# First stage of a convolution and SwiGLU block: modulation vectors and token scaling moved from TensorE and VectorE to ScalarE, a new written order, and a bank of its own for the last half tile

## The chip, the cores and the metric

The kernel runs on one core of one Trainium2 chip. The core has five engines with instruction queues of their own: TensorE (PE, matrix products into PSUM banks), VectorE (DVE), ScalarE (ACT), GpSimd (POOL) and SyncE (SP, which here only issues transfers). Each queue is worked through in order; an instruction waits for semaphores that others raise. The metric is the device time of one execution in microseconds (us), as a median of runs.

## The reference

One layer (DEPTH is 1) over 1024 tokens of width 1024, in float32:

```python
sh1, sc1, g1, sh2, sc2, g2 = split(silu(c) @ ada_w + ada_b, 6)   # 1024 values each
h  = rmsnorm(x, norm1_g) * (1 + sc1) + sh1
gate_b, gate_c, hv = split(h @ conv_w_in, 3)                     # 1024 x 3072
y  = (gate_b * conv3_grid(gate_c * hv, conv_w)) @ conv_w_out
x  = x + g1 * y
h2 = rmsnorm(x, norm2_g) * (1 + sc2) + sh2
gate, up = split(h2 @ ffn_w_in, 2)                               # 1024 x 5632
x  = x + g2 * ((silu(gate) * up) @ ffn_w_out)
out = rmsnorm(x, final_g)
```

## The kernel before

Every large product is done on operands of the type that the profile calls fp32r, each split into a high part (a cast, on ACT) and a low part (the rest, a subtraction on DVE): three matmuls stand for one, high x high, low x high and high x low (TERMS). The large products also use a Strassen-like scheme with seven instead of eight block products, which is why tiles are called P1 to P7, S1 to S4, 11, 12, 21 and 22.

**The first stage** is what the change is about. It makes `sh1` and `sc1`, and with them the first products of `h @ conv_w_in`, for the first 512 tokens and for seven output blocks of 128 columns (the pairs in EARLY), each in a PSUM bank of its own (tile `x` in the profile). It goes through the width in eight steps, k = 0 to 7, of 128 rows of the product. Step k needs

- `ada[k]`: the 1024 rows of `ada_w` for 128 entries each of shift and scale, 1 MB, loaded on SP's queue in four transfers (`Ada.load`). Its sum over 8 blocks of rows, weighted with silu(c), is made in two accumulators: blocks 0 and 1 on ACT (`ada_acc`, L161), the others on DVE (L165), one addition of the two accumulators (L77), and the rest on PE: `total` sums over partitions by matmuls of one column (L179), of the merged accumulator (`ones`) and, from k = 1, of block 7 left out of the sums (`direct`; the factor is then a column of `cols`). Two entries, shift and scale, make 4 matmuls per step, and the profile shows each as two.
- `columns` (L184, L186, on DVE): scale1 and shift1, 128 values each, from the PSUM result.
- the token values of the step: xT is modulated with them, `A11h` or `A12h` (high, on ACT, L729), `xT` again in full precision (DVE, L314) and `A11l` or `A12l` (low, DVE, L74).
- the weights `w0r` (458 KB, SP's queue) and their parts `w0h` (ACT, L358) and `w0l` (DVE, L74).

The stage's order is written out by hand, for PE, ACT, DVE and SP: a loop over k, in which a list of (pair, terms) sets the order of the 21 matmuls. `by_term` does seven pairs' high x high, then seven low x high, then seven high x low; after the fourteenth (n == 14) the next step's `total` and `tokens` are written, so that they run while PE does the last seven. Steps 3 and 7 use `by_half`, with `total` earlier. After step 3 the seven banks hold P1, which ACT copies out (`save_p1`, L372) and POOL's queue stores to memory (`aside`, L373). Loads for step k+3 are issued at the start of step k; after the loads of the eight steps come the other 512 tokens (x) and the weights `wf` of five more blocks. PE then goes on without a break in those blocks (L410) and in the stage called Mixes (L460).

**The end.** The last product P4 is accumulated in four banks (`zs`). Three token tiles are finished first; the fourth, in `LastTile`, is done in two halves of 256 columns, both in the same bank, so that the first half's scaling runs beside the second half's matmuls. `rest` then takes the root of the sum of squares (`rsqrt`: ACT's root, and a Newton step on DVE), scales both halves of the row and writes them.

## Time and profile before

| | |
|---|---|
| median of 3 runs | 1000.98 us (1000.25 to 1001.6) |
| profiled execution | 1000.51 us, its span 998.7 us |
| PE busy | 983.7 us, 98% of the span, 4426 matmul records |
| DVE, ACT, POOL busy | 718.4, 482.3, 102.7 us |
| DMA, mean over the span | 181 GB/s |
| first stage (16.6 to 66.4 us): PE, DVE, ACT busy | 48.7, 41.0, 29.1 of 49.8 us |

The page counts an engine as busy while it computes; of a 998.7 us span PE is idle for 15.0 us. Rows of the timeline give start, length, engine, line, operation, tiles, and in brackets how long the engine stood idle before the instruction and what ended that.

### The profile page before, as it was taken

How to read it: one execution, taken by the hardware profiler on the slowest of the kernel's cores; microseconds unless marked ns; L12 is line 12 of the kernel's file. 1: busy time of each engine (PE TensorE's matmuls, PEld its weight loads, DVE VectorE, ACT ScalarE, POOL GpSimd, SP SyncE). 2: the span in 40 equal slices, each digit the busy share in tenths (PEclk: the TensorE clock that was granted, in tenths of full speed). 3: DMA queues.
4: the chain of work that ended last, by engine and by line, in shares of the span. 5: the costliest groups of instructions: out<-in, count | busy, mean ns of one | idle time of the engine just before them, and what ended most of it. 6: DMA issues, size and time to landing. Idle time of an engine off the chain costs nothing.

```text
span 998.7 us, 12313 instructions
## 1 busy us (share of the span) xinstructions
PE 983.7 (98%) x4426; PEld 809.2 (81%) x4426; DVE 718.4 (72%) x1038; ACT 482.3 (48%) x766; POOL 102.7 (10%) x183
## 2 busy tenths in 40 slices
PE   8999999999999999999999999999999999999996
PEld 6788888887788878888888888888888888888885
DVE  5877988888746799787665665665665755878885
ACT  6555876675435675243333333333334353535553
POOL 2131001110111210110110110110110110000000
PEclk9999999999999999999999999999999999999999
DMA  9997489996784232545431431431316954577533
GB/s 298 321 349 243 135 260 268 279 296 194 242 235 148 85 107 84 161 156 153 133 116 53 148 116 53 146 108 63 127 56 211 376 196 155 176 261 277 185 123 133
DMA packets 155325, 180.46 MB, mean 181 GB/s; under 512 B 8020, under 2 KB 112576, under 8 KB 155264
## 3 DMA queue, kind: packets, MB, share of 16 engines
q1 hardware_dynamic: 141584, 135.81, 43.5%
q0 software_dynamic: 12448, 40.69, 12.7%
q10 hardware_dynamic: 1232, 3.18, 0.8%
q8 instruction: 34, 0.56, 0.2%
q14 instruction: 27, 0.22, 0.1%
HBM read 135.33 MB, written 38.03 MB: 174 GB/s over the span
## 4 chain that ended last, share of the span: by engine, by line
PE 93%; DVE 2%; DMA 2%; ACT 1%; issue 1%; POOL 0%; ACTq 0%; DVEq 0%; POOLq 0%
PE X_f L570 23%; PE zP L1384 21%; PE m L460 16%; PE Z_f L570 12%; PE y L1014 7%; PE Y_f L570 6%; PE x L368 3%; PE x L410 3%; PE xT L295 1%; DMA vl_t<-vd 1%; PE ada_ps L179 1%; PE x1T L987 1%; DMA rows<-in_norm_g_dram 1%; DMA wr_f<-in_ffn_w_in_dram 1%; PE ada_ps L244 0%
## 5 line engine op out<-in xcount | busy, mean ns | idle before, releaser
L74 DVE TENSOR_TENSOR BP_f<-wr_f,BP_f 128x512 fp32r<-128x512 f32 x154 | 105.0, 687 | 60.7 <-ACT BP_f L83 58.8
L83 ACT CAST BP_f<-wr_f 128x512 fp32r<-128x512 f32 x154 | 94.2, 620 | 87.0 <-PE Z_f L570 55.9
L1384 PE MATMUL zP<-w3l_P,a3h_P 128*128 128x512 f32 (+1 forms) x319 | 121.8, 382 | 0.0
L1384 PE MATMUL zP<-w3h_P,a3l_P 128*128 128x512 f32 (+1 forms) x319 | 121.8, 382 | 0.0
L1384 PE MATMUL zP<-w3h_P,a3h_P 128*128 128x512 f32 (+1 forms) x319 | 120.4, 382 | 0.6 <-DVE bot L80 0.6
L1384 PEld LDWEIGHTS zP<-w3h_P,a3h_P 128*128 128x128 f32 x319 | 60.0, 188 | 12.5 <-DVE bot L80 0.8
L1384 PEld LDWEIGHTS zP<-w3h_P,a3l_P 128*128 128x128 f32 x319 | 60.0, 188 | 11.6
L1384 PEld LDWEIGHTS zP<-w3l_P,a3h_P 128*128 128x128 f32 x319 | 60.0, 188 | 11.5
L74 DVE TENSOR_TENSOR a3l_P<-a3l_P,a3h_P 128x1024 fp32r<-128x1024 f32 (+1 forms) x42 | 47.4, 1134 | 24.8 <-ACT a3h_P L1239 24.8
L570 PE MATMUL X_f<-A11h,BP_f 128*128 128x512 f32 x176 | 57.7, 390 | 0.0
L570 PE MATMUL X_f<-AS3h,BP_f 128*128 128x512 f32 x176 | 57.7, 389 | 0.0
L570 PE MATMUL Z_f<-AS4h,BP_f 128*128 128x512 f32 x176 | 57.6, 389 | 0.0
L570 PE MATMUL X_f<-AS2h,BP_f 128*128 128x512 f32 x176 | 57.6, 389 | 0.0
L570 PE MATMUL X_f<-A22h,BP_f 128*128 128x512 f32 x176 | 57.6, 389 | 0.0
L570 PE MATMUL Y_f<-A12h,BP_f 128*128 128x512 f32 x176 | 57.5, 389 | 0.0
L570 PE MATMUL Z_f<-AS1h,BP_f 128*128 128x512 f32 x176 | 57.4, 389 | 0.0
L1014 PE MATMUL y<-woh,vh_t 128*128 128x512 f32 x128 | 50.5, 394 | 0.0
L1014 PE MATMUL y<-woh,vl_t 128*128 128x512 f32 x128 | 49.9, 390 | 0.0
L1014 PE MATMUL y<-wol,vh_t 128*128 128x512 f32 x128 | 49.9, 390 | 0.0
L1239 ACT CAST a3h_P<-a3l_P 128x1024 fp32r<-128x1024 f32 (+1 forms) x42 | 40.7, 978 | 14.4 <-DMA a3l_P<-ad_S 7.9
L74 DVE TENSOR_TENSOR wr_f<-wr_f,wr_f 128x512 f32<-128x512 f32 x66 | 45.2, 688 | 1.5
L77 DVE TENSOR_TENSOR u_f<-Z_f,u_f 128x512 f32<-128x512 f32 x22 | 15.2, 690 | 37.5 <-ACT u_f L587 34.8
(310 smaller groups left out, 2331.9 us busy)
## 6 DMA issues: line engine op xcount, KB each, us to landing
wr_f<-in_ffn_w_in_dram SPq DMA_DIRECT2D x44, 512.0 KB, 4.4
ada_w<-in_ada_w_dram SPq DMA_DIRECT2D x64, 256.0 KB, 6.0
w_P<-in_ffn_w_out_dram SPq DMA_DIRECT2D x30, 512.0 KB, 5.9
a3l_P<-ad_S SPq DMA_DIRECT2D x20, 512.0 KB, 6.4
ad<-a POOLq DMA_DIRECT2D x33, 256.0 KB, 2.6
ada_w<-in_ada_w_dram SPq DMA_DIRECT2D x16, 512.0 KB, 4.8
a3l_P<-ad SPq DMA_DIRECT2D x15, 512.0 KB, 3.9
wr<-in_conv_w_in_dram SPq DMA_DIRECT2D x12, 512.0 KB, 6.2
```

The costliest lines, as they stand in the source:

```text
L74: return nc.vector.tensor_tensor(o, a, b, op=ALU.subtract)
L77: return nc.vector.tensor_tensor(o, a, b, op=ALU.add)
L83: nc.scalar.copy(hi, raw)
L179: nc.tensor.matmul(self.ps[j][:, j:j + 1], lhsT=part[:, j, :], rhs=by, start=i == 0, stop=i == n - 1)
L295: nc.tensor.transpose(self.ps[g][:, i * P:(i + 1) * P], self.x[:, k * P:(k + 1) * P], ident)
L368: nc.tensor.matmul(xbank[pair], lhsT=w0[k][wi][:, place[pair], :], rhs=h_of(k, 0)[hi], start=(k == 0 and i == 0), stop=(k == KD - 1 and i ...
L410: nc.tensor.matmul(xbank[self.pair], lhsT=self.w[wi][:, k, :], rhs=h_of(half * KH + k, 0)[hi], start=(half == 0 and k == 0 and i == 0), st ...
L460: nc.tensor.matmul(self.ps[a], lhsT=self.w[pname][wi][:, k, a * P:(a + 1) * P], rhs=A[aname, k // 2][hi][:, k % 2, :], start=(q == 0 and k ...
L570: mm = nc.tensor.matmul(ps, lhsT=w[:, wi, 2 * kp + kk, :], rhs=A[aname, kp][hi][:, kk, :], start=(first and kp == 0 and kk == 0 and i == 0 ...
L1014: mm = nc.tensor.matmul(ys[t][n], lhsT=vt[t][vi][:, k, :], rhs=wo[k][wi][:, n * H:(n + 1) * H], start=(k == 0 and i == 0), stop=(k == KD - ...
L1239: nc.scalar.copy(hi, f(lo))
L1384: mm = nc.tensor.matmul((zs[t] if to is None else to)[:, cols], lhsT=a[ai][:, k % 2, t * P:(t + 1) * P], rhs=w[wi][:, k % 2, cols], start= ...
```

## The change

In the first stage:

- `Ada` is made with `direct` 2 for k = 1 and 0 for the later steps (1 before): step 1 has 6 one-column matmuls instead of 4, steps 2 to 7 have 2 each. The block of rows that PE no longer sums is one more instruction on DVE (L165 before, L167 now).
- scale1 and shift1 are made on ACT (two activations with a scale and a bias per partition; a new constant `gab1`, made once on DVE), the full-precision token values too.
- The order is new. ACT's two sums stand four matmuls earlier than before; DVE has `w0l` of the next step first, then three sums, the low part of the tokens, three sums and the merge. Steps 3 and 4 have orders of their own (`first_five`, `first_four`): two or three pairs are kept back and done whole after `total`.
- P1 is stored from SP's queue, behind the loads of the stage, instead of from POOL's queue. The tiles that hold it live longer.
- The scaling, squares and weights for the blocks that follow stand at other places.

At the end: the second half of the last tile gets a bank `zl` of its own. What P1, P6 and P7 left for that half in the old bank is multiplied with g2 and added to x1 beforehand (two DVE instructions of 128x256). `rsqrt` is a root, a reciprocal, one combined instruction and a second reciprocal, which gives half the value (the factor 2 is put into `fg`); for the last tile the root takes the addition of the two sums in as its bias.

PE's order where step 2 ends and the total for step 3 is made (`x` are the seven banks, `ada_ps` the bank of the totals), before:

```order
L368 MATMUL x_1_311<-A11l_121,w0h_331 128x512
L179 MATMUL ada_ps<-cols,ada_w_353 128x1
L179 MATMUL ada_ps<-ones,ada_acc_348 128x1
L179 MATMUL ada_ps<-cols,ada_w_353 128x1
L179 MATMUL ada_ps<-ones,ada_acc_348 128x1
L368 MATMUL x_2_299<-A11h_120,w0l_332 128x512
```

and with the change:

```order
L370 MATMUL x_2_310<-A11l_123,w0h_338 128x512
L370 MATMUL x_1_312<-A11l_123,w0h_338 128x512
L181 MATMUL ada_ps<-ones,ada_acc_352 128x1 x2
L370 MATMUL x_2_300<-A11h_122,w0l_339 128x512
L370 MATMUL x_1_302<-A11h_122,w0l_339 128x512
```

The two matmuls with `ada_w` and `cols` are gone, and the other two stand side by side.

ACT's order from the values of step 3 to those of step 5 (`p` are the copies of P1, `A12h` the high part for step 4 where it first stands), before:

```order
L729 ACTIVATE A11h_120<-xT_1_109,shift_105,scale_104 128x512
L358 CAST w0h_448<-w0r_367 128x896
L372 COPY p_0_486<-x_2_299 128x512
L372 COPY p_0_486<-x_1_301 128x512
L372 COPY p_2_495<-x_2_303 128x512
L161 ACTIVATE ada_acc_412<-ada_w_414,cols 128x256
L161 ACTIVATE ada_acc_413<-ada_w_414,cols 128x256
L729 ACTIVATE A12h_118<-xT_2_110,shift_105,scale_104 128x512
L372 COPY p_2_495<-x_1_305 128x512
```

and with the change:

```order
L757 ACTIVATE xT_1_111<-xT_1_111,shift_107,scale_106 128x512
L360 CAST w0h_453<-w0r_371 128x896
L163 ACTIVATE ada_acc_415<-ada_w_417,cols 128x256
L163 ACTIVATE ada_acc_416<-ada_w_417,cols 128x256
L376 COPY p_0_491<-x_2_300 128x512
L186 ACTIVATE scale_106<-ada_ps,gab_89,cols 128x1
L188 ACTIVATE shift_107<-ada_ps,cols 128x1
L748 ACTIVATE A12h_120<-xT_2_112,shift_107,scale_106 128x512
L376 COPY p_0_491<-x_1_302 128x512
L376 COPY p_2_505<-x_2_304 128x512
L757 ACTIVATE xT_2_112<-xT_2_112,shift_107,scale_106 128x512
L376 COPY p_2_505<-x_1_306 128x512
```

Two copies now stand between the high part and the full values of step 4, and one ahead of scale and shift; the sums for step 5 stand ahead of all of them.

DVE's order from the merge of the sums for step 4 to the low part of step 4's tokens (`A12l`), before:

```order
L77 TENSOR_TENSOR ada_acc_359<-ada_acc_359,ada_acc_360 128x256
L765 COPY xT_0_108<-h_279 128x512
L165 SCALAR_TENSOR_TENSOR ada_acc_412<-ada_w_414,cols,ada_acc_412 128x256
L165 SCALAR_TENSOR_TENSOR ada_acc_413<-ada_w_414,cols,ada_acc_413 128x256
L184 TENSOR_SCALAR scale_104<-ada_ps,ab_88,cols 128x1
L186 TENSOR_SCALAR shift_105<-ada_ps,cols 128x1
L165 SCALAR_TENSOR_TENSOR ada_acc_412<-ada_w_417,cols,ada_acc_412 128x256
L165 SCALAR_TENSOR_TENSOR ada_acc_413<-ada_w_417,cols,ada_acc_413 128x256
L314 TENSOR_SCALAR xT_2_110<-xT_2_110,scale_104,shift_105 128x512
L74 TENSOR_TENSOR A12l_119<-xT_2_110,A12h_118 128x512
```

and with the change:

```order
L77 TENSOR_TENSOR ada_acc_363<-ada_acc_363,ada_acc_364 128x256
L74 TENSOR_TENSOR w0l_454<-w0r_371,w0h_453 128x896
L167 SCALAR_TENSOR_TENSOR ada_acc_415<-ada_w_417,cols,ada_acc_415 128x256
L167 SCALAR_TENSOR_TENSOR ada_acc_416<-ada_w_417,cols,ada_acc_416 128x256
L167 SCALAR_TENSOR_TENSOR ada_acc_415<-ada_w_420,cols,ada_acc_415 128x256
L74 TENSOR_TENSOR A12l_121<-xT_2_112,A12h_120 128x512
```

scale, shift and xT are gone from DVE; `w0l` of step 4 stands here instead of later, and three sums instead of four ahead of the low part.

The diff, cut to its core:

```diff
     ab1 = cst.tile([P, 6 * KD], F32, name="ab1")
+    gab1 = cst.tile([P, KD], F32, name="gab1")
...
+        mul(gab1, ab1[:, KD:2 * KD], g1c)
...
         def columns(self):
             k = self.k
-            nc.vector.tensor_scalar(scale1[:, k:k + 1], self.ps[1][:, 1:2], ab1[:, KD + k:KD + k + 1], g1c[:, k:k + 1],
-                                    op0=ALU.add, op1=ALU.mult)
-            nc.vector.tensor_scalar(shift1[:, k:k + 1], self.ps[0][:, 0:1], ab[:, k:k + 1], None, op0=ALU.add)
+            nc.scalar.activation(scale1[:, k:k + 1], self.ps[1][:, 1:2], AF.Identity, scale=g1c[:, k:k + 1],
+                                 bias=gab1[:, k:k + 1])
+            nc.scalar.activation(shift1[:, k:k + 1], self.ps[0][:, 0:1], AF.Identity, bias=ab[:, k:k + 1])
...
+    def store_p1():
+        for pair, tile in p1_left:
+            nc.sync.dma_start(aside[PAIRS.index(pair)], tile)
...
-                ada.append(Ada(k, 1))
+                ada.append(Ada(k, 2 if k == 1 else 0))
...
+        def rows_ahead(k):
+            if k < KD:
+                ada[k].sums(2, 3, 4)
+
+        def rows_first(k):
             if k < KD:
                 ada[k].sums(0, 1, scalar=True)
-                ada[k].sums(2, 3)
+
+        def rows_left(k):
+            if k < KD:
+                ada[k].sums(*range(5, KD - ada[k].direct))
+                ada[k].merge()
 
         def tokens(k):
-            after = ada[k + 1] if k + 1 < KD else None
             if k:
                 ada[k].columns()
-                nc.scalar.activation(*(h_of(k, 0)[0], xT[0][k // 2][:, k % 2, :], AF.Identity),
+                nc.scalar.activation(h_of(k, 0)[0], xT[0][k // 2][:, k % 2, :], AF.Identity,
                                      scale=scale1[:, k:k + 1], bias=shift1[:, k:k + 1])
-            if after:
-                if k != KH:
-                    high0(k + 1)
-                after.sums(4, 5)
+            low0(k)
+            rows_ahead(k + 1)
+
+        def tokens_low(k):
             if k:
-                modulate1(k, 0, vector=True)
+                o = xT[0][k // 2][:, k % 2, :]
+                nc.scalar.activation(o, o, AF.Identity, scale=scale1[:, k:k + 1], bias=shift1[:, k:k + 1])
                 low1(k, 0)
...
+        first_five, first_four = [[(pair, (i,)) for i in range(3) for pair in EARLY[:n]] +
+                                  [(pair, range(3)) for pair in EARLY[n:]] for n in (5, 4)]
+        orders = [by_term] * (KH - 1) + [first_five, first_four] + [by_term] * (KH - 2) + [by_half]
+        total_at = [14] * (KH - 1) + [11, 12] + [14] * (KH - 1)
...
+            for n, (pair, terms) in enumerate(orders[k]):
+                if n == total_at[k] - 4:
+                    rows_first(k + 2)
+                if n == total_at[k] and not last:
                     ada[k + 1].total()
                     tokens(k + 1)
+                    if k != KH - 1:
+                        tokens_low(k + 1)
+                if n == 13 and k == KH - 1:
+                    tokens_low(KH)
                 term0(k, pair, terms)
...
-    def rsqrt(s, name):
-        r, e = tiny(f"{name}_r"), tiny(f"{name}_e")
-        nc.scalar.activation(r, s, AF.Sqrt)
-        nc.vector.reciprocal(r, r)
-        nc.vector.scalar_tensor_tensor(e, r, r, s, op0=ALU.mult, op1=ALU.mult)
-        nc.vector.tensor_scalar(e, e, -0.5, 1.5, op0=ALU.mult, op1=ALU.add)
-        mul(r, r, e)
+    def root_of(s, name, **plus):
+        q = tiny(f"{name}_q")
+        nc.scalar.activation(q, s, AF.Sqrt, **plus)
+        return q
+
+    def rsqrt(s, name, q):
+        r = tiny(f"{name}_r")
+        nc.vector.reciprocal(r, q)
+        nc.vector.scalar_tensor_tensor(q, r, s, q, op0=ALU.mult, op1=ALU.add)
+        nc.vector.reciprocal(r, q)
         return r
...
-        def __init__(self, t, zs):
-            self.t, self.zs, self.zf = t, zs, t2("zf")
+        def __init__(self, t, z):
+            self.t, self.zs, self.zf = t, [z, bank("zl")], t2("zf")
+            c = self.columns(1)
+            mul(bot[t][:, c], z[:, c], g2[:, c])
+            add(x1b[t][:, c], x1b[t][:, c], bot[t][:, c])
...
+            q = root_of(self.ss[1], "zl", bias=self.sums)
             add(s, self.ss[1], self.sums)
-            r = rsqrt(s, "zl")
+            r = rsqrt(s, "zl", q)
...
-                        mm = steps(TH - 1, k, cols=slice(i * H // 2, (i + 1) * H // 2))
+                        mm = steps(TH - 1, k, last.zs[1] if i else None, last.columns(i))
```

More of the change, by code (lines that the diff above doesn't have):

```diff
@@ L788, in trunk_kernel @@
                 next_loads(3)
-            if k == KD - 3:
-                xs[TH].squares()
-            elif k == KD - 2:
-                more[0].weights(0)
+            if k == KD - 2:
                 xs[TH + 1].squares()
-                for i in range(2):
-                    xs[TH + i].scale()
+                xs[TH].scale()
         cols2 = columns_of("cols2", 4 * KD, rows2)
```

62 lines of the change are left out of this document (34 added, 28 removed).

## The prediction

> **What bounds the kernel now.** The page's head, and its busy times:
>
> ```profile
> span 998.7 us, 12313 instructions
> PE 983.7 (98%) x4426; PEld 809.2 (81%) x4426; DVE 718.4 (72%) x1038; ACT 482.3 (48%) x766; POOL 102.7 (10%) x183
> ```
>
> PE is idle for 998.7 - 983.7 = 15.0 us in all. So a change gains by taking work off PE, by closing some of these gaps, or by shortening what comes after the last matmul. PE's waits name the two largest gaps that it touches:
>
> ```profile
> PE zP L1384 <- DVE bot L80: 0.6, 1, 0.6
> PE x L368 <- ACT A12h L729: 0.5, 1, 0.5
> ```
>
> That leaves out short stalls between matmuls of one group, so I read the first stage from PE's timeline, at the first group of each step (k = 0 to 7), with the total between step 2 and step 3:
>
> ```profile
> 16.61 1.89 PE L368 MATMUL x<-A11h,w0h 128*128 128x512 f32 x7 [0.44 <-ACT A11h L323]
> ...
> 23.35 1.89 PE L368 MATMUL x<-A11h,w0h 128*128 128x512 f32 x7
> ...
> 29.18 1.78 PE L368 MATMUL x<-A11h,w0h 128*128 128x512 f32 x7
> ...
> 32.66 0.28 PE L179 MATMUL ada_ps<-cols,ada_w 128*128 128x1 f32 x2
> 32.80 0.36 PE L179 MATMUL ada_ps<-ones,ada_acc 128*128 128x1 f32 x2
> 33.02 0.36 PE L179 MATMUL ada_ps<-cols,ada_w 128*128 128x1 f32 x2
> 33.24 0.36 PE L179 MATMUL ada_ps<-ones,ada_acc 128*128 128x1 f32 x2
> 33.47 1.88 PE L368 MATMUL x<-A11h,w0l 128*128 128x512 f32 x7
> 35.19 1.76 PE L368 MATMUL x<-A11h,w0h 128*128 128x512 f32 x7
> ...
> 41.96 2.43 PE L368 MATMUL x<-A12h,w0h 128*128 128x512 f32 x7 [0.52 <-ACT A12h L729]
> ...
> 48.36 1.78 PE L368 MATMUL x<-A12h,w0h 128*128 128x512 f32 x7
> ...
> 54.10 1.78 PE L368 MATMUL x<-A12h,w0h 128*128 128x512 f32 x7
> ...
> 59.84 1.76 PE L368 MATMUL x<-A12h,w0h 128*128 128x512 f32 x7
> ```
>
> Steps 5 and 6 take 5.74 us each (48.36, 54.10, 59.84) without a stall. The seven steps from 16.61 to 59.84 take 43.23 us; 7 x 5.74 is 40.18, so 3.05 us are stalls, most in step 0 (6.74) and around P1 (steps 3 and 4: 6.77 and 6.40).
>
> **The change part by part.** *Matmuls off PE.* A total's four parts start at 32.66, 32.80, 33.02 and 33.24, the next group at 33.47: the first costs 0.14, each further one 0.22 to 0.23. Six totals lose two: 6 x 0.45 = 2.7 us. Step 1's gains two: 0.45. Net **-2.25 us** (-2.0 if the switch between operand types weighs more in the short block). An unstalled step then takes 5.74 - 0.45 = 5.29 us.
>
> *ACT's new share.* These are ACT's rows in the stage (sums of two blocks, high part, weights' cast, P1's copies, and a copy out of PSUM):
>
> ```profile
> 31.88 0.91 ACT L161 ACTIVATE ada_acc<-ada_w,cols 128x256 f32<-128x256 f32 x2 [0.86 <-DMA ada_w<-in_ada_w_dram]
> 34.08 0.82 ACT L729 ACTIVATE A11h<-xT,shift,scale 128x512 fp32r<-128x512 f32 x1 [1.29 <-DVE shift L186]
> 34.83 0.94 ACT L358 CAST w0h<-w0r 128x896 fp32r<-128x896 f32 x1
> ...
> 41.82 2.03 ACT L372 COPY p<-x 128x512 f32<-128x512 f32 x4
> ...
> 62.09 0.59 ACT L384 COPY c<-x 128x512 f32<-128x512 f32 x1 [0.97 <-PE x L368]
> ```
>
> No row has a one-column activation with scale and bias read per partition. I build it: 128x512 with both costs 0.82, a copy of that size 0.59, so 0.11 or 0.12 per such operand; a bare one-column activation at the end of the kernel is 0.21 (below). Scale, with two, 0.44; shift, with one, 0.32; successive ones overlap by 0.1 (four copies of 0.59 in 2.03): **0.66 us for the pair** (estimate). Bounds: 0.42, DVE's pair now (from 33.64 below to A11h's start at 34.08, less a hop), and 0.76 without overlap. ACT's step is 0.91 + 0.66 + 0.82 + 0.72 (xT, overlapping) + 0.94 = 4.05 of 5.29 us.
>
> The Trainium skill's page "ScalarE: Activation LUTs", section "Rules for kernel authors", puts add and mul on VectorE rather than ScalarE. The rows agree that the move is dearer in itself (0.82 against DVE's 0.55 below); by that rule the change should lose where ACT sets the pace, and that is the first rival.
>
> *The loop of one step* in the new order: total, ACT's pair (0.66), high part (0.82), xT, DVE's low part, three sums, merge, next total. DVE's durations:
>
> ```profile
> 28.81 0.88 DVE L165 SCALAR_TENSOR_TENSOR ada_acc<-ada_w,cols,ada_acc 128x256 f32<-128x256 f32 x2 [0.76 <-DMA ada_w<-in_ada_w_dram]
> ...
> 31.30 0.43 DVE L77 TENSOR_TENSOR ada_acc<-ada_acc,ada_acc 128x256 f32<-128x256 f32 x1
> 31.65 1.08 DVE L74 TENSOR_TENSOR w0l<-w0r,w0h 128x896 fp32r<-128x896 f32 x1
> ...
> 33.64 0.28 DVE L184 TENSOR_SCALAR scale<-ada_ps,ab,cols 128x1 f32<-128x1 f32 x1
> ...
> 34.94 0.55 DVE L314 TENSOR_SCALAR xT<-xT,scale,shift 128x512 f32<-128x512 f32 x1
> 35.52 0.69 DVE L74 TENSOR_TENSOR A11l<-xT,A11h 128x512 fp32r<-128x512 f32 x1
> ```
>
> 0.66 + 0.82 + 0.72 + 0.69 + 3 x 0.44 + 0.43 + 0.37 (the total) + hops of some 0.05 gives about 5.1, under 5.29 by 0.2. DVE's own work is 1.0 + 6 x 0.44 + 0.62 + 0.4 = 4.7. So PE keeps the pace wherever nothing else comes in; high parts are ready 1.53 after the total, and PE has 1.7 of w0l matmuls to cover them.
>
> *The walk, step by step,* with loads landing as now (ACT's sums for step 4 end waiting for a load at 31.88, DVE's fourth sum for step 3 at 28.81):
> - Step 0 starts 0.15 later (pair on ACT, uncovered): 16.76. w0l is now split before the sums, so the waits around 20 to 23 us shrink: 6.34, next start 23.1.
> - Step 1: 5.3, to 28.4. Step 2: DVE's low part waits behind the sum released at 28.81 and is just in time (29.95 for 30.0). The total is over at 32.1, but ACT sits in the sums till 32.79, so the high part is ready at 34.15: start 34.2, length 5.8.
> - Step 3 has five matmuls before the low part is needed (35.35), and it is there at 35.65; the total waits for the merge till 37.4. Length 5.96, to 40.16.
> - Step 4: ACT does copy, pair, high part, two copies, xT, copy. The fourth bank's copy ends at 41.6, PE wants that bank at 40.85: 0.8 stalled. Length 6.14, to 46.3.
> - Steps 5 and 6: 5.3 each, to 56.9, where 59.84 stands now.
>
> That is 2.94 us; the matmuls are 2.25 of it, so **stalls give -0.7** (3.05 now, 2.3 with the late start). The end points: all new stalls vanish (-2.3 more), or twice as many (+2.3).
>
> *P1 on SP's queue* costs nothing: the stores are issued behind the stage's loads, where SP has issued all that PE waits for, and ahead only of Mixes' first weights. Those come 3 to 4 us later at worst (seven issues of the 0.5 to 0.6 us that POOL's took). Their first reader is DVE's wr row at 91.37; without the work before it, this would cost up to those 4 us. The stores as they are now, and that reader:
>
> ```profile
> 38.69 1.73 POOL L373 DMA_DIRECT2D aside<-p  x3 [27.48 <-ACT p L372]
> 42.68 2.13 POOL L373 DMA_DIRECT2D aside<-p  x4 [2.26 <-ACT p L372]
> ...
> 91.37 1.22 DVE L74 TENSOR_TENSOR wr<-wr,wr 128x1024 f32<-128x1024 f32 x1
> ```
>
> Loads issued around 40 us can land sooner without them; I count nothing for it, as the wait at 31.88 is the last one on a load in the stage. The other moves (squares, scaling, gab1) lie beside PE.
>
> *The last half tile*, from PE's timeline, DVE's, and the chain of waits:
>
> ```profile
> 985.97 0.28 PE L1384 MATMUL zP<-w3h_P,a3l_P 128*128 128x256 f32 x1
> 986.82 0.39 PE L1384 MATMUL zP<-w3h_P,a3h_P 128*128 128x256 f32 x1 [0.57 <-DVE bot L80]
> 987.04 0.28 PE L1384 MATMUL zP<-w3l_P,a3h_P 128*128 128x256 f32 x1
> ...
> 989.09 0.75 DVE L1332 SCALAR_TENSOR_TENSOR bot<-bot,z_r,fg 128x512 f32<-128x512 f32 x1
> ...
> 992.54 0.17 DVE zl_s L77
> ...
> 992.73 0.21 ACT zl_r L1290
> ...
> 993.42 0.16 DVE zl_e L1293
> ```
>
> Matmuls start 0.12 apart; this one starts 0.73 late and holds the next 0.10 longer: **-0.83 us**, if DVE, with two more instructions of some 0.35 before 980, is free by 990.2 (its last epilogue now ends at 989.84, one instruction shorter per root then). *The root*: the sum ahead of it (0.17 + 0.02) goes beside it; two DVE instructions (0.16 and 0.17, with gaps) become one: **-0.37**, or -0.2 if the bias costs the root 0.1 and the reciprocal more.
>
> **Sum**: -2.25 - 0.7 - 0.83 - 0.37 = -4.15 us. The profiled execution took 1000.51 us (1.8 outside its span); the median is 0.47 above it. So 1000.98 - 4.15 = **996.8 us**, a ratio of 0.996.
>
> **The rivals.**
> 1. *ACT binds around P1* (what the page's rule would give). For: in steps 3 to 5 ACT has seven copies besides (3.5 us) and stands in order behind loads. Against: ACT has room, as its waits in steps 4 to 7 show:
>
> ```profile
> ACT A12h L729 <- DVE shift L186: 9.0, 4, 3.3
> ```
>
>    If the stalls there double (+2.3) and the later steps recover nothing: -4.15 + 2.3, 999.1; with PE's saved matmuls standing as stalls too, 1.2 left: 999.8.
> 2. *Handed back in Mixes.* There DVE is full:
>
> ```profile
> 100.00:125.00 25.00, 25.00 (x112) 20.72 (x111) 25.00 (x25) 20.65 (x28) 1.78 (x2) 1.00 0.48 134
> ```
>
>    If DVE's stretch starts no earlier, PE waits for it, and only the end's 1.2 us remains: 999.8. Against: the splits before that stretch follow copies of finished banks, which PE's progress releases, so they come earlier with it.
> 3. *Slower: ACT's pair sets the step.* If the pair costs p instead of 0.66, the loop is 5.1 + (p - 0.66); it decides from p = 0.85, and passes the old 5.74 at 1.3. At p = 2.0 seven steps of 6.44 lose 4.9, less 1.2 at the end: 1004.7. For it: no row has such an activation on a bank just written. Against: the copy out of PSUM at 62.09 has no such excess.
> 4. *The change doesn't do what it says*: the second half still waits, since DVE is late with the last tiles: 0.83 is lost, 997.6.
>
> **How the numbers follow.** Forecast 0.70 with rival 4 in it, rival 1 0.14, rival 2 0.10, rival 3 0.06. The forecast's own bounds: -2.25 - 2.3 - 0.83 - 0.4 = -5.8 (995.2), and -2.0 + 0.7 (half the doubling) - 0.2 = -1.5 (999.5). Range 995.2 to 999.7: rivals 1 and 2 lie at its edge, half in; 3 is out. About 0.2% (2 us) is what a measurement here tells from no change: faster than 999.0 in all of the forecast but its edge, and some of rival 1: 0.77; within 0.2%: 0.18; slower: 0.05.
>
> **What would show it.** Right: totals of two parts about 0.4 us long; steps 5 and 6 near 5.3 us; the first group of step 7 near 56.9; PE's list without the wait for A12h over 0.8 and without zP on bot; the last matmul group ending some 0.8 sooner beyond the stage's 2.9. Wrong: PE waiting for ACT's high part in each step (rival 1 or 3, by the length of L186 and L188), or PE waits for w0l or BP tiles between 100 and 135 us (rival 2), or stalls longer than 1 us at step 4, or loads that ACT or DVE waits for after 40 us.

## The result: 0.5% faster, a little more than forecast

| | median, us | single executions |
|---|---|---|
| kernel before | 1000.50 | six, 999.51 to 1001.6 |
| changed kernel | 994.85 | six, 994.5 to 996.16 |

The ratio is 0.9946, with a 95% interval of 0.9933 to 0.9958. The forecast was 996.8, with a range from 995.2: the direction was right, and the time lies 0.35 us below the range. The profiled execution took 995.36 us. The head of its page:

```profile
span 993.6 us, 12268 instructions
PE 979.7 (99%) x4406; PEld 805.7 (81%) x4406; DVE 712.8 (72%) x1015; ACT 490.9 (49%) x789; POOL 99.6 (10%) x176
```

PE is busy for 4.0 us less (20 matmul records fewer, and short stalls that the page counts as busy), and idle for 13.9 us instead of 15.0. ACT has 8.6 more, as it now makes the columns and the full token values. PE's waits:

```profile
PE x1T L1014 <- DVE xr L1066: 1.0, 1, 1.0
PE xT L297 <- DVE x L291: 1.0, 2, 0.6
PE x L370 <- ACT p L376: 0.5, 1, 0.5
```

The wait for A12h and the one of zP on bot are gone; a wait for a copy of P1 has come. PE's timeline at the first group of each step, with the total of step 3:

```profile
16.27 2.77 PE L370 MATMUL x<-A11h,w0h 128*128 128x512 f32 x7
...
23.47 1.78 PE L370 MATMUL x<-A11h,w0h 128*128 128x512 f32 x7
...
28.76 1.78 PE L370 MATMUL x<-A11h,w0h 128*128 128x512 f32 x7
...
31.99 0.50 PE L181 MATMUL ada_ps<-ones,ada_acc 128*128 128x1 f32 x4
32.36 1.87 PE L370 MATMUL x<-A11h,w0l 128*128 128x512 f32 x7
34.06 1.32 PE L370 MATMUL x<-A11h,w0h 128*128 128x512 f32 x5
...
40.01 0.84 PE L370 MATMUL x<-A12h,w0h 128*128 128x512 f32 x3
41.35 0.50 PE L370 MATMUL x<-A12h,w0h 128*128 128x512 f32 x1 [0.50 <-ACT p L376]
...
46.09 1.75 PE L370 MATMUL x<-A12h,w0h 128*128 128x512 f32 x7
...
51.35 1.77 PE L370 MATMUL x<-A12h,w0h 128*128 128x512 f32 x7
...
56.61 1.78 PE L370 MATMUL x<-A12h,w0h 128*128 128x512 f32 x7
```

A total holds PE for 0.37 (31.99 to 32.36), unstalled steps take 5.26 to 5.30, and step 7 starts at 56.61 where the prediction had 56.9. But step 0 took 7.20, and its first group 2.77 instead of 1.78. The view by stretches tells why (columns: stretch, its length, busy time of PE, its weight loads, DVE, ACT and POOL, the clock granted to TensorE, DMA share, GB/s); the changed kernel:

```profile
14.00:20.00 6.00, 6.00 (x22) 4.06 (x22) 4.26 (x9) 4.57 (x12) 0.00 (x0) 0.72 1.13 362
20.00:60.00 40.00, 39.36 (x187) 31.37 (x186) 30.36 (x59) 30.47 (x57) 1.92 (x4) 1.00 0.91 291
```

and the kernel before:

```profile
14.00:20.00 6.00, 5.56 (x29) 4.16 (x29) 3.80 (x10) 4.18 (x8) 0.00 (x0) 1.00 1.18 305
20.00:60.00 40.00, 38.95 (x191) 31.03 (x190) 33.84 (x73) 21.11 (x36) 5.39 (x9) 1.00 1.11 331
```

Two things are to be seen. In this execution of the changed kernel the clock was halved for a while around the first group (the mean granted clock is 0.72 over these 6 us; the trace's clock records have 0.50 from 14.80 to 18.21 us). And the loads run at 362 GB/s where the kernel before has 305, though both issue the same transfers there, in the same order, on the same queue. The second is a gain that the prediction has no term for. With the starts of the stages in the timelines, and a second profile of the unaltered changed kernel (g1 below) whose clock was full, the account is, in us:

| stretch | before | changed | changed, g1 | forecast |
|---|---|---|---|---|
| to the first group | 16.61 | -0.34 | -0.23 | +0.15 |
| first group to step 7 | 43.23 | -2.89 | -3.71 | -3.09 |
| step 7 to Mixes | 36.26 | -0.07 | -0.05 | 0 |
| Mixes to PE's half tiles | 886.04 | -0.65 | -0.74 | 0 |
| half tiles to the end | 16.60 | -1.24 | -1.23 | -1.20 |
| span | 998.7 | -5.2 | -6.0 | -4.15 |

Over all timings of the study the kernel before has a mean of 1000.21 us (68 executions) and the changed one 994.99 (16). So the first three executions, with a median of 1000.98, stood 0.8 high, and the change is worth 5.2 us (5.1 to 5.5 where the two kernels were timed side by side).

### The profile page after: what moved, and what is told of

It is laid out like the page before. It is cut to its first block, busy times and chain, and to the rows that moved or that the text cites. A ratio compares the mean times of both kernels' runs of the same rounds, so it can differ in the third digit from the quotient of the medians.

```text
span 993.6 us, 12268 instructions
## 1 busy us (share of the span) xinstructions
PE 979.7 (99%) x4406; PEld 805.7 (81%) x4406; DVE 712.8 (72%) x1015; ACT 490.9 (49%) x789; POOL 99.6 (10%) x176
## 4 chain that ended last, share of the span: by engine, by line
PE 94%; DVE 2%; DMA 1%; ACT 1%; issue 0%; POOL 0%; SPq 0%; POOLq 0%; DVEq 0%; ACTq 0%
PE X_f L581 24%; PE zP L1422 21%; PE m L471 17%; PE Z_f L581 12%; PE y L1041 7%; PE Y_f L581 6%; PE x L370 3%; PE x L421 3%; DVE BP_f L74 1%; PE x1T L1014 1%; DMA x<-in_x_dram 1%; PE ada_ps L181 0%; PE xT L297 0%; PE zl L1422 0%; DMA vl_t<-vd 0%
## 5 line engine op out<-in xcount | busy, mean ns | idle before, releaser
L1422 PE MATMUL zP<-w3h_P,a3l_P 128*128 128x512 f32 (+1 forms) x308 | 118.6, 385 | 0.0
L1422 PE MATMUL zP<-w3l_P,a3h_P 128*128 128x512 f32 (+1 forms) x308 | 118.6, 385 | 0.0
L1422 PE MATMUL zP<-w3h_P,a3h_P 128*128 128x512 f32 (+1 forms) x308 | 117.2, 385 | 0.0
L1422 PEld LDWEIGHTS zP<-w3h_P,a3h_P 128*128 128x128 f32 x308 | 57.9, 188 | 11.7
L1422 PEld LDWEIGHTS zP<-w3l_P,a3h_P 128*128 128x128 f32 x308 | 57.9, 188 | 11.6
L1422 PEld LDWEIGHTS zP<-w3h_P,a3l_P 128*128 128x128 f32 x308 | 57.9, 188 | 11.4
```

What stands on the lines that cost most here:

```text
L1422: mm = nc.tensor.matmul((zs[t] if to is None else to)[:, cols], lhsT=a[ai][:, k % 2, t * P:(t + 1) * P], rhs=w[wi][:, k % 2, cols], start= ...
```

## The experiments

Most of the reading is of one table: how long each step takes on PE, from the starts of its first groups (clock: whether the granted clock fell to 0.50 inside step 0; tiles: on a multiple of 256 bytes or not, explained under "The place of the tiles").

| kernel | clock fell | tiles | first group | steps 0 to 6 |
|---|---|---|---|---|
| before | no | off | 16.61 | 6.74 5.83 6.01 6.77 6.40 5.74 5.74 |
| e2 | yes | off | 16.39 | 7.42 5.72 5.74 6.78 6.40 5.71 5.75 |
| e7 | yes | off | 16.30 | 7.41 5.73 5.73 6.78 6.42 5.71 5.70 |
| f1 | yes | on | 16.31 | 6.79 5.78 5.72 6.78 6.39 5.73 5.70 |
| changed | yes | on | 16.27 | 7.20 5.29 5.30 5.95 6.08 5.26 5.26 |
| g1 (changed) | no | on | 16.38 | 6.38 5.29 5.30 5.95 6.06 5.26 5.28 |
| h4 (changed) | no | on | 16.19 | 6.41 5.30 5.30 5.94 6.08 5.26 5.31 |
| e1 | no | on | 16.56 | 6.39 5.27 5.27 5.99 6.07 5.25 5.28 |
| e3 | no | on | 16.70 | 6.39 5.74 5.75 6.18 6.51 5.70 5.76 |
| e4 | no | on | 16.79 | 6.41 5.52 5.55 6.23 5.96 5.26 5.52 |
| e5 | no | on | 17.93 | 6.41 5.29 5.28 5.97 6.08 5.26 5.31 |
| e6 | yes | on | 16.31 | 7.30 5.31 5.31 5.51 6.37 5.26 5.27 |
| f2 | yes | off | 16.71 | 7.20 5.31 5.27 5.95 6.09 5.25 5.30 |
| f3 | no | off | 16.60 | 6.36 5.34 5.77 6.10 6.04 5.26 5.30 |
| h2 | yes | off | 16.45 | 7.30 5.29 5.33 5.94 6.08 5.26 5.26 |
| h3 | no | off | 16.97 | 6.40 5.30 5.27 5.98 6.08 5.26 5.30 |
| g2 | yes | on | 16.17 | 7.87 5.30 5.27 5.97 5.58 5.26 5.30 |
| g3 | no | on | 16.69 | 6.39 5.26 5.29 5.52 6.05 5.26 5.26 |
| h1 | yes | on | 16.55 | 7.77 5.29 5.27 5.47 5.65 5.32 5.28 |
| i1 | no | on | 19.17 | 6.40 5.32 5.29 5.50 5.65 5.31 5.27 |

### The two halves of the change

e1 is the changed kernel without its end (the diff up to `rsqrt` alone):

> The changed first stage with the old end of the kernel. The two profiled executions differ by 5.15 us: 0.34 before the first group of the stage (16.61 to 16.27), 2.88 up to the first L410/L421 product, 0.08 more up to Mixes, 0.65 in single stalls between 248 and 365 us, and 1.2 at the end. Theory A (what stood in the prediction, the two extras being chance of load arrivals): this kernel gains 2.9 to 3.2 us, ratio 0.9970, and its first group starts anywhere between 16.2 and 16.7. Theory B (the stage causes the extras too): it gains 3.9 to 4.4, ratio 0.9958, the first group stands at 16.3 and no stall shows near 251 us.

995.71 us against 1000.34, ratio 0.9952 (0.994 to 0.9965): 4.6 us, so theory B, though its first group stands at 16.56 and not at 16.3. The stage alone brings more than the 2.9 that the walk gave.

e2 is the other half, the old stage with the new end:

> The old first stage with the changed end. Theory A: a gain of 1.1 to 1.2 us (0.82 for the bank, 0.3 to 0.4 for the root), ratio 0.9988, and since nothing ahead of the end differs from the kernel before, its first group and its stalls at 254 and 317 us show what differs by chance between two executions (first group between 16.2 and 16.7). Theory B: the same gain, with the first group at 16.6 and the stall of 0.3 at 254.5 as in the kernel before. Rival 4 of the prediction (the second half still waits) would leave 0.3.

999.50 against 1000.34, ratio 0.999 (0.9981 to 0.9999): 0.84 us, less than the 1.1 to 1.2 expected, but the interval holds these too. Its first group stands at 16.39, and no stall shows at 254 us, so that one came by chance. e7 takes the end apart, with the bank and the old `rsqrt`:

> The kernel before with the bank for the last half tile alone, and the root as it was. The whole changed end gave 0.84 in the medians and 1.1 in the profile, against the prediction's 1.2. If the prediction's terms hold: 0.83 here (999.4), PE's last matmul 0.8 earlier after the start of the half tiles, and the root 0.3 to 0.4 beside it. If the root's shorter form was part of what frees DVE in time: the second half starts late again, and less than 0.5 is gained.

999.30 against 1000.09, with an interval that holds 1 (0.9986 to 1.0004), so this one rests on the profile. From the first half tile's start PE's last matmul comes 7.79 us later in e7 (982.01 to 989.80) and 8.62 in the kernel before (982.14 to 990.76): 0.83 for the bank, as forecast. What follows shows in DVE's rows; e7:

```profile
990.12 0.21 DVE L1359 TENSOR_SCALAR zl_sums<-zl_ss,parts 128x1 f32<-128x1 f32 x1 [0.40 <-ACT x L1355]
990.25 0.41 DVE L80 TENSOR_TENSOR bot<-zl,g 128x256 f32<-128x256 f32 x1
```

and the changed kernel, with the whole new root:

```profile
984.60 0.21 DVE L1389 TENSOR_SCALAR zl_sums<-zl_ss,parts 128x1 f32<-128x1 f32 x1
...
986.30 0.42 DVE L80 TENSOR_TENSOR bot<-zl,g 128x256 f32<-128x256 f32 x1 [0.63 <-PE zl L1422]
...
988.09 0.17 DVE L1322 RECIPROCAL zl_r<-zl_q 128x1 f32<-128x1 f32 x1 [0.17 <-ACT zl_q L1316]
988.29 0.22 DVE L1323 SCALAR_TENSOR_TENSOR zl_q<-zl_r,zl_s,zl_q 128x1 f32<-128x1 f32 x1
988.54 0.17 DVE L1324 RECIPROCAL zl_r<-zl_q 128x1 f32<-128x1 f32 x1
988.74 0.49 DVE L1398 TENSOR_SCALAR zf<-zf,zl_r 128x512 f32<-128x512 f32 x1
```

With the old root DVE stands behind `zl_sums`, which waits for ACT, and begins on the last half 0.45 after the start of PE's last matmul; with the new one it waits for PE alone and begins 0.31 after it (0.32 in the kernel before). From there to the final scaling it is 2.44 us (986.30 to 988.74), against 2.72 before (991.08 to 993.80): 0.28 for the root itself. The rest of the 1.24 in the account lies behind the scaling, in the last transfer.

### What in the stage brings it

e3 puts one block of rows back on PE in steps 2 to 7:

```diff
-                ada.append(Ada(k, 2 if k == 1 else 0))
+                ada.append(Ada(k, 2 if k == 1 else 1))
```

> The changed kernel, with one block of rows per entry back on PE in steps 2 to 7 (12 one-column matmuls more, six sums fewer on DVE). If PE's matmuls were what the change took off the path, the loss is 6 x 0.45 = 2.7 us (997.5; steps 5 and 6 at 5.74 again). If the gain came from the order and from what DVE lost, the loss is under 1 us, and the steps stay below 5.5.

997.23 us, 2.4 above the changed kernel, and the steps without a stall (1, 2, 5 and 6) are back at 5.70 to 5.76. So PE's matmuls are the largest single part of the gain.

e4 makes scale and shift on DVE again (the two old instructions of `columns`):

> The changed kernel, with scale and shift made on DVE again (token values stay on ACT). The prediction priced the pair at 0.66 on ACT; the profile shows 0.54 from the start of scale to the start of the high part, against 0.50 from DVE's scale in the kernel before. If PE keeps the pace (steps of 5.27), the place of the pair is worth nothing: within 0.3 us of the changed kernel. If relieving DVE was needed, the pair stands behind the merge and w0l on DVE's queue and the steps grow to 5.6 or more: 2 us lost.

996.03, about 1.1 above the changed kernel: PE keeping the pace was not enough, and the second theory was nearer, with half its price. The rows of DVE around the total of step 2 in e4:

```profile
26.07 0.43 DVE L77 TENSOR_TENSOR ada_acc<-ada_acc,ada_acc 128x256 f32<-128x256 f32 x1
27.20 0.28 DVE L186 TENSOR_SCALAR scale<-ada_ps,ab,cols 128x1 f32<-128x1 f32 x1 [0.70 <-PE ada_ps L181]
27.39 0.21 DVE L188 TENSOR_SCALAR shift<-ada_ps,cols 128x1 f32<-128x1 f32 x1
27.52 1.08 DVE L74 TENSOR_TENSOR w0l<-w0r,w0h 128x896 fp32r<-128x896 f32 x1
```

and in the changed kernel:

```profile
26.08 0.43 DVE L77 TENSOR_TENSOR ada_acc<-ada_acc,ada_acc 128x256 f32<-128x256 f32 x1
26.42 1.08 DVE L74 TENSOR_TENSOR w0l<-w0r,w0h 128x896 fp32r<-128x896 f32 x1
```

With the pair in its queue DVE stands for 0.70 until PE's total is there, and `w0l` starts 1.10 later; three steps then take 5.52 to 5.55 instead of 5.3, and step 3 takes 6.23 instead of 5.95, and PE's list of waits has 0.4 for A11l. The pair on ACT costs next to nothing more than on DVE, in the changed kernel's rows:

```profile
27.24 0.35 ACT L186 ACTIVATE scale<-ada_ps,gab,cols 128x1 f32<-128x1 f32 x1 [1.47 <-PE ada_ps L181]
27.49 0.25 ACT L188 ACTIVATE shift<-ada_ps,cols 128x1 f32<-128x1 f32 x1
27.77 0.82 ACT L748 ACTIVATE A11h<-xT,shift,scale 128x512 fp32r<-128x512 f32 x1
```

It is 0.53 from scale to the high part, against 0.44 from DVE's scale to A11h in the kernel before (33.64 to 34.08). So the rule of the Trainium skill's page "ScalarE: Activation LUTs", section "Rules for kernel authors", that add and mul belong on VectorE, goes the wrong way here by some 1.1 us, although DVE's pair is the shorter one (0.44 against 0.53): what counted is whose queue had to stand still for PE. The pair on DVE at another place, behind `w0l`, was not tried, so the 1.1 us belongs to this place in its queue.

e6 gives steps 3 and 4 the old lists:

```diff
-        orders = [by_term] * (KH - 1) + [first_five, first_four] + [by_term] * (KH - 2) + [by_half]
-        total_at = [14] * (KH - 1) + [11, 12] + [14] * (KH - 1)
+        orders = [by_term] * (KH - 1) + [by_half] + [by_term] * (KH - 1) + [by_half]
+        total_at = [14] * (KH - 1) + [10] + [14] * KH
```

> The changed kernel with the kernel before's lists for steps 3 and 4 (by_half with the total after ten matmuls, by_term). The prediction gives the new lists part of its stalls' 0.7: step 3 went from 6.77 to 5.97, step 4 from 6.40 to 6.08, and a step without a stall takes 5.27. If the lists did that, the two steps take 0.6 to 1.1 us more here. Rival (DVE's new order and the columns on ACT did it): less than 0.3 us more.

The two steps take 11.88 instead of 12.01 to 12.03, so the new lists bring nothing on PE's timeline; what else in the order shortens the two steps was not taken apart. (The median, 995.64, is of executions from 994.5 to 996.26, and step 0 of the profiled one fell into a halved clock.)

e5 stores P1 from POOL's queue (`save_p1` without `later=True`):

> The changed kernel, with P1 stored from POOL's queue right after each copy, as in the kernel before. The prediction counted the move at nothing: within 0.3 us of the changed kernel (994.6 to 995.2). Rival: between 38 and 48 us the stores share the engines with the loads of steps 6 and 7 and of x, and those come later by what 1.8 MB take, some 5 us; if ACT, DVE or PE then wait for a load after 45 us, 0.5 to 1 us is lost. If the stall near 313 us (0.7 in the changed kernel, 0.85 and 1.2 with the old first stage) belongs to POOL's queue, it grows to 0.8 or more here.

Each step is the changed kernel's within 0.05, and the stall near 313 us is 0.70, beside 0.68 there: nothing for the move, as forecast, and the rival falls. The median of 996.06 is that of four executions from 994.93 to 996.40; the profiled one came to its first group late, at 17.93 (16.17 to 16.97 in the other kernels with the changed stage, i1 aside), ahead of every store. The clock did that: its transposes, e5's first and then e1's,

```profile
9.23 5.58 PE L297 MATMUL xT<-ident,x 128*128 128x128 f32 x32
```

```profile
8.84 4.60 PE L297 MATMUL xT<-ident,x 128*128 128x128 f32 x32
```

start 0.21 us apart until 13.07 us in e5 and until 10.55 in e1, and 0.11 apart from there on; the records of the granted clock begin with full speed at 13.15 and 10.76. Whether the time differs by the move is not settled by these executions.

### The place of the tiles

The rate of the loads differs from the first microseconds on, before any changed instruction runs. What differs there is where the tiles lie. Constants stand ahead of all other tiles in each partition's memory, and the new one, `gab1`, is 8 values or 32 bytes wide. By the built programs' addresses, the large tiles of the kernel before start 224 bytes past a multiple of 256, and those of the changed kernel on one (those that the stage's loads write lie on multiples of 512 as well). f1 gives the kernel before these 32 bytes, and nothing else; the tile `parts` is not used beyond its old width:

```diff
-    parts = cst.tile([P, 2 * NT], F32, name="parts")
+    parts = cst.tile([P, 2 * NT + 8], F32, name="parts")
```

> The kernel before, with the constant tile parts 32 bytes per partition wider (never read or written there), so that every large tile starts on a multiple of 256 bytes of its partition, as in the changed kernel, where the 32 bytes of gab1 do it; in the kernel before they start 224 past one. Theory C (place of the tiles): between 10 and 16 us a 512-byte packet takes 27 ns instead of 33, the loads run at some 350 GB/s instead of 305 to 315, and the time falls by 0.9 to 1.5 us (998.8 to 999.4), the part of the gain that the prediction has no term for. Theory N (the faster loads come from the new order, from engines that read less beside them): packets stay at 33 ns and the time at 1000.3.

The other four are the changed kernel, with 56, 8, 16 and 32 columns more in the same place, and a control:

> The changed kernel, with parts 224 bytes wider, so that its tiles start 224 bytes past a multiple of 256, as in the kernel before. Theory C: 512-byte packets take 33 ns again, ACT's sums wait for loads, and 0.9 to 1.5 us are lost (995.8 to 996.4), about the prediction's 4.15 below the kernel before. Theory N: 27 ns, and the time of the changed kernel (994.9).

> The changed kernel, with parts 32 bytes wider, so that its tiles start 32 bytes past a multiple of 256. Theory C1 (what counts is into how many pieces the packet is cut): the Trainium skill's page DMA: Bandwidth & Descriptors, section How a descriptor splits into AXI transactions, has a descriptor that starts off a 256-byte boundary begin with a transaction from the boundary below; by it 512 bytes cost 17 beats of 32 bytes at 32 past the boundary, 23 at 224 past it and 16 on it. Under C1 packets take 27 to 29 ns here and the time is that of the changed kernel within 0.4 us. Theory C2 (any start off the boundary costs the same): 33 ns, and 995.8 to 996.4 us.

> The changed kernel with parts 64 bytes wider: tiles start 64 past a multiple of 256. With 32 and with 224 past it, 512-byte packets took 32 and 33 ns, on it 27. If any start off the 256 costs (the packet touches three pieces of 256 instead of two), 32 to 33 ns here and in the next kernel, and 0.5 to 1 us above the unaltered one in this call. If only starts off 64 cost, 27 ns, and no loss.

> The same with 128 bytes: 27 ns if a start on 128 is enough, 32 to 33 if the boundary that counts is 256; time as in the kernel with 64.

> The changed kernel unaltered, beside the others of this call: 27 ns, 994.3 to 995.5.

The mean length of a 512-byte packet that starts between 10 and 30 us (8,900 to 10,000 of them in each trace's records), and the times:

| kernel | start past a multiple of 256 | 512-byte packet | median, us |
|---|---|---|---|
| before | 224 | 32.9 ns | 1000.10 beside f1 |
| f1 | 0 | 27.2 | 999.29 |
| changed; h4 | 0 | 27.1; 27.1 | 994.85; 994.92 |
| f3 | 32 | 31.8 | 995.84 |
| h2 | 64 | 31.9 | 995.85 |
| h3 | 128 | 32.5 | 995.45 |
| f2 | 224 | 32.8 | 995.52 |

Theories C and C2: in these loads each of the four starts off the boundary costs 4.7 to 5.8 ns a packet. So a start on 128 is not enough; whether 256 is, or 512 is needed, no run tells, as none moves the tiles by 256. The Trainium skill's page "DMA: Bandwidth & Descriptors", section "How a descriptor splits into AXI transactions", has the boundary at 256, and the runs agree as far as they go; its count of beats, by which 32 past it would cost one beat in 16 and 224 past it seven, does not give the price: 4.7 and 5.7 ns.

The price holds for loads that follow each other closely. Between 500 and 700 us all 512-byte packets are those of `wr_f`, the core moves 100 GB/s, and a packet takes 28.3 ns in the kernel before, 28.3 in f1 and 27.9 in the changed kernel: there the place of the tiles costs nothing that shows. The DMA view over 2 to 38 us agrees with the table; the kernel before, then f1:

```profile
DMA packets 16078, 11.26 MB, mean 313 GB/s; under 512 B 725, under 2 KB 15572, under 8 KB 16075
```

```profile
DMA packets 18185, 12.44 MB, mean 346 GB/s; under 512 B 800, under 2 KB 17683, under 8 KB 18182
```

In time, the 19 executions of the four shifted kernels have a mean of 995.71, the 16 of the unaltered one 994.99: 0.72 us (standard errors 0.08 and 0.15). Timed side by side, h2 and h3 have a mean of 995.69, and h4 994.96. In the kernel before, the 32 bytes alone bring 0.8 in the medians (999.29 against 1000.10) and 0.5 in the means; the interval of that ratio (0.9986 to 1.0003) holds 1, so there the gain in time is not shown.

f3 shows where it goes. ACT's rows in its step 2, in which the prediction had a stall:

```profile
31.87 0.91 ACT L163 ACTIVATE ada_acc<-ada_w,cols 128x256 f32<-128x256 f32 x2 [1.22 <-DMA ada_w<-in_ada_w_dram]
32.69 0.33 ACT L186 ACTIVATE scale<-ada_ps,gab,cols 128x1 f32<-128x1 f32 x1
32.92 0.25 ACT L188 ACTIVATE shift<-ada_ps,cols 128x1 f32<-128x1 f32 x1
33.20 0.82 ACT L748 ACTIVATE A11h<-xT,shift,scale 128x512 fp32r<-128x512 f32 x1
```

The sums stand in wait for their load till 31.87 (the prediction had them end at 32.79; they do at 32.78), the pair comes late behind them, and PE starts step 3 at 34.07 (predicted: 34.2):

```profile
34.07 0.73 PE L370 MATMUL x<-A11h,w0h 128*128 128x512 f32 x2 [0.31 <-ACT A11h L748]
```

With tiles on the boundary the load is there in time, and step 2 takes 5.30 instead of 5.77; the same sums in g1, without a wait:

```profile
29.46 0.90 ACT L163 ACTIVATE ada_acc<-ada_w,cols 128x256 f32<-128x256 f32 x2
```

Over the whole stage the list of ACT's waits, from 16 to 62 us, has for f3

```profile
ACT ada_acc L163 <- DMA ada_w<-in_ada_w_dram: 3.5, 4, 1.2
```

and 1.5, 1.1 and 0.4 us for h2, f2 and h3. With tiles on the boundary the line is gone (changed, g1, h4), and so it is from the kernel before (2.6 us) to f1. Where step 0 was lengthened by the clock (f2, h2) or started late (h3), the loads had time to catch up, and the stall is missing too.

### The clock

> The changed kernel, unaltered, beside the others of this call. Of the changed stage's four kernels with tiles on multiples of 256, two executions had a TensorE clock of 0.50 granted for some 3.4 us around the first group (step 0 of 7.20 us), two had not (6.39 and 6.41). Theory D (the clock's dip comes and goes by execution, worth 0.8 us where it meets step 0): 994.5 to 996.2 in the single runs, and in the profile step 0 is either 6.4 or 7.2, the steps after it 5.27, 5.3, 5.97, 6.08, 5.25, 5.28 each within 0.05. Theory E (the dip belongs to the kernel): 7.2 again.

Theory D: step 0 took 6.38. The granted clock of g1:

```profile
14.00:20.00 6.00, 5.53 (x29) 4.10 (x28) 4.15 (x8) 4.67 (x12) 0.00 (x0) 1.00 1.13 362
```

The falls in the other profiles last 3.41 us each and begin at 8.0 and 8.3 us (where PE mostly waits) or between 14.8 and 16.8 us, and nine of the twenty profiles have none; in step 0 a fall costs 0.7 to 1.5 us (e2 against the kernel before, g2 against g1). Of the changed kernel the two profiled executions without one took 994.30 and 994.55 us, the one with it 995.36; how much of the spread of its single executions (994.28 to 996.16) the clock makes is not shown, since the others have no trace. i1 tries to fill PE ahead of it, on top of h1 (below):

```diff
             for g in range(2):
                 xs[i].transposes(g)
+            if 0 < i < TH - 1:
+                keep_busy(i, 2 * P)
```

> The kernel of h1 (old lists for steps 3 and 4, two of P1's copies on DVE), with three idle matmuls of 128x256 among the transposes ahead of the first step, where PE waits 0.4 and 0.6 us for x. In 9 of 16 changed or unchanged kernels' profiles so far the clock granted falls to 0.50 for 3.41 us between 8 and 20 us, and step 0 then takes 7.2 to 7.9 instead of 6.4. The Trainium skill's page TensorE: Matmul & The Clock Gate, section Part 1: The HAM clock gate, lays such a fall to a window of 3.41 us with too little work in it. Theory: with PE fuller from 10 to 13 us no fall comes, step 0 takes 6.4, steps 3 and 4 together 11.1: 993.5 to 994.0 in most runs. Rival (the thin window is the one of the one-column matmuls at 13 to 15 us, or one that wide waits do not decide): falls as often as before, 994.3 to 995.4.

(Miscounted there: it was ten of eighteen.) No fall in its profile, but the fastest and slowest of five executions are 993.9 and 996.42, the median 995.43, and its first group stands at 19.17. In e5, where the clock also came up at 13.1 us and no idle matmuls stand between the transposes, it is 17.93: the idle matmuls delay the start by 1.2 us there, as much as a fall costs. One profile without a fall, where nine of twenty have none, does not tell whether PE's idle time decides. In the 3.41 us ahead of each of the nine later falls PE waits for 0.71 us at most at a stretch, and g1, without a fall, has a wait of 0.6 too.

### Versions that might beat both

All three take P1's copies off ACT at step 4, where PE waits 0.50 for one. g2 makes the third copy on DVE:

```diff
-    def save_p1(pair, tile, later=False):
-        nc.scalar.copy(tile, xbank[pair])
+    def save_p1(pair, tile, later=False, vector=False):
+        (nc.vector.tensor_copy if vector else nc.scalar.copy)(tile, xbank[pair])
...
-                save_p1(pair, kept[n // 2][:, n % 2, :], later=True)
+                save_p1(pair, kept[n // 2][:, n % 2, :], later=True, vector=n == 2)
```

> The changed kernel, with the third of P1's seven copies made on DVE, which stands idle for 1.56 us there waiting for the full values of step 4. PE waits 0.50 us for the copy of the fourth bank (41.35). If that copy is late only because ACT has three copies and the pair ahead of the full values, the wait goes and with it 0.4 to 0.6 us (994.3). Rival (the low part or the step after takes it back): the same wait at A12l or at the next total, and the time of the changed kernel within 0.2 us.

g3 has also another list for step 3: seven, then five low x high, total after 13:

> As the one before, and in step 3 all seven high x high products come first (five in the changed kernel), so that the low part has two matmuls more of cover. The changed kernel's row of step 3 shows 0.14 us of stall ahead of the first A11l product and 0.15 ahead of the total: if these go, 0.2 to 0.4 us beside the other gain (994.0). Rival (the merge is the limit, ready at 37.1): the total waits as before, and nothing is gained beside the other.

h1 has the old lists of e6, with `vector=n in (3, 4)`:

> The changed kernel with the kernel before's lists for steps 3 and 4 (they took 5.51 and 6.37 us with the new rest, against 5.95 and 6.08 of the new lists), and the fourth and fifth of P1's copies on DVE. The old lists' step 4 waits 0.70 for a copy of ACT's; with two copies fewer, ACT has the full values of step 4 about 1 us sooner and the last copy by 41.1. Theory (ACT's copies are the only limit left there): steps 3 and 4 take 5.5 and 5.3 to 5.5, 1.0 to 1.2 less than in the changed kernel: 993.8. Rival (DVE's two copies make the low part late): a wait for A12l of 0.3 or more, and a gain under 0.6.

Steps 3 and 4 take 11.55, 11.57 and 11.12, against 12.01 to 12.03. In g3 the wait only moved from step 3 to step 4 (5.52 and 6.05). h1 comes nearest to two steps without a stall (10.6); DVE's rows there:

```profile
40.03 1.28 DVE L376 COPY p<-x 128x512 f32<-128x512 f32 x2
41.43 0.69 DVE L74 TENSOR_TENSOR A12l<-xT,A12h 128x512 fp32r<-128x512 f32 x1
```

The low part starts only behind the two copies, so PE's first product with it stands 1.92 after the start of step 4 (42.27), where step 3 has 1.63. The times are 994.46, 994.71 and 994.97, beside 994.93 and 994.92 for the changed kernel: 0.9 us on PE's timeline in h1, but no difference that five executions resolve when a fall of the clock in step 0 weighs as much. A version that beats the changed kernel is not shown.

## Why the prediction was nearly right, and where it was not

- *Matmuls off PE* (-2.25, step 5.29): right. Steps without a stall take 5.25 to 5.31 (changed, g1, h4, e1), and e3 gives 2.4 back.
- *ACT's pair* (0.66, bounds 0.42 to 0.76): 0.53. The start was to come 0.15 later; it varies by more than that between executions (16.19 to 16.38 in three of the changed kernel, 17.93 in e5 with the late clock).
- *The walk* (first group to step 7 in 40.14 us): 40.17 in f3, the one profile with the old place of the tiles, a full clock and a usual start. Single steps agree within 0.15 there. (h3, also with a full clock but started 0.4 later, took 39.59, without the stall in step 2; so the agreement holds for the start that the walk assumed.) With the tiles moved it is 39.52 and 39.60 (g1, h4): the loads come sooner, and the stall that the walk has in step 2 is gone.
- *Stalls around P1* (5.96 and 6.14): 5.95 and 6.06. The new lists were not their cure, though (e6).
- *P1 on SP's queue* (0): right in each step, not settled in time.
- *The last half tile* (-0.83): 0.83. *The root* (-0.37): 0.28, and without it 0.13 of the bank's gain goes to the wait behind `zl_sums`.
- *Rivals*: ACT does not bind, its scale waits for PE's total in five steps (this is the changed kernel from 16 to 62 us):

```profile
ACT scale L186 <- PE ada_ps L181: 8.2, 5, 2.5
```

  Nothing is handed back in Mixes (the lead grows from 3.30 to 3.95 us between its start and the half tiles), the pair is far from 1.3, and the half tile does not wait.

**The step that failed** is the assumption of the walk, "with loads landing as now", and with it the sentence that counted `gab1` among the moves that "lie beside PE". As an instruction it does. As a tile of 32 bytes it moves every tile behind it, and the loads with them: 0.72 us. The rest of the miss is in the base and in one stretch without a term. The three executions shown stood 0.8 above the mean of 68, so that -4.15 from 1000.21 would have been 996.1. And between Mixes and the half tiles 0.65 us (0.74 in g1) went that no step had: from the first Mixes product to the first product of X_f with AS2h near 519 us it is 422.9 to 423.0 us in the kernel before, e2 and e7, 422.4 in f1, and 422.0 to 422.5 in each kernel with the new stage, tiles on the boundary or off it. A part of it shows at x1T: near 365 us it starts 1.47 to 1.57 after the matmul ahead of it in the first three and 1.35 to 1.39 in the others, and near 317 us 0.85, 1.22 and 1.18 in the first three and 0.38 to 0.87 in the others. What brings it stays open, since the new stage with shifted tiles has it, and f1 too. With 0.65 for that and 0.72 for the tiles, 996.1 becomes 994.7; the mean of the changed kernel is 994.99.

The range was missed by the base. As a change, 5.2 us lies inside its bounds of 1.5 to 5.8: counted from 1000.21 its lower end is 994.4, and from 1000.98 it is 995.2. But the bound of 5.8 lets every stall of the stage vanish, and those around P1 did not: steps 3 and 4 still take 12.0 us, where 10.6 would be without a stall. The faster loads and the 0.65 behind the stage, which had no term, filled the gap.

## What to carry to other kernels

A new tile, however small, moves the tiles behind it: compare addresses, and where loads that the kernel waits for follow each other closely, keep the tiles that they write in rows of 512 bytes on multiples of 512 bytes, as here (256 may do, no run tells); it was worth 0.7 us. Time the base as often as the change: here 0.8 us of the miss lay in a median of three. A short instruction can be better placed on an engine whose next work waits for the same event than on the one that is fastest at it (here 1.1 us). And before effects of half a microsecond are compared, look at the granted clock of each profile: a fall in step 0 cost 0.7 to 1.5 us here, more than most of them.

## What the hardware showed that was not expected

- Between 10 and 30 us, where loads run at 307 to 360 GB/s, a 512-byte packet into a tile on a multiple of 256 bytes (here of 512 too) took 27.0 to 27.4 ns, and 31.8 to 32.9 ns at 32, 64, 128 or 224 past it; one of 1536 bytes took 65.6 to 68.9 and 75.2 to 75.7. At 100 GB/s the difference was gone (28.3 and 27.9 ns).
- TensorE's clock comes up to full speed between 4.6 and 13.2 us, and until then transposes start 0.21 us apart instead of 0.11 (e5, e1). Then, in eleven of the twenty profiles, the granted clock falls once more to 0.50, for 3.41 us, with the start between 8.0 and 16.8 us; it does so in some executions of a kernel and not in others. The Trainium skill's page "TensorE: Matmul & The Clock Gate", section "Part 1: The HAM clock gate", has such a window of 3.41 us that runs free of the kernel's start, and calls the effect run-variable; the lengths and the two executions of one kernel agree.
